# A transformer kernel on one core: the byte offsets of the k-tiles of x^T and of the activations

## The chip, the core and the metric

One core of a Trainium2 chip runs the whole program. Its engines are TensorE (PE in the rows, with its weight loads shown apart as PEld), VectorE (DVE), ScalarE (ACT), GpSimd (POOL) and SyncE (SP), which issues the transfers. The metric is the device time of one execution in microseconds, as the median of a few runs.

## The reference, cut to what matters

Two transformer blocks run one after the other on 256 tokens of width 2048, all in 32-bit floats. Nearly all of the work is products of a token matrix with a large weight matrix:

```
def first_block(x, ...):
    h = rmsnorm(x, pre_mix_g);  proj = h @ w_in          # 2048 -> 4368
    ...two attentions...
    x = x + rmsnorm(concat(o_a, o_b) @ w_out, post_mix_g)
    h = rmsnorm(x, pre_ffn_g)
    u = causal_dwconv(h @ w_up, conv_w, conv_b)          # 2048 -> 11264
    gate, val = split(u)
    x = x + rmsnorm((gelu(gate) * val) @ w_down, post_ffn_g)   # 5632 -> 2048
def second_block(x, c, ctx, ...):
    h  = modulate(rms_norm(x));  hc = modulate(rms_norm(ctx))
    q, k, v, u = h @ w_in_2;     kc, vc = hc @ w_in_2
    x = x + g_a * (concat(attention, pool(u)) @ w_out_2)
    x = x + g_m * (square(relu(modulate(rms_norm(x)) @ w_mlp_up)) @ w_mlp_down)   # 2048 -> 8192 -> 2048
    return rms_norm(x)
```

## The kernel before

Each 32-bit operand is split in two parts of type fp32r, a rounded `hi` and a remainder `lo`, and a product is three matmuls: hi·hi, hi·lo and lo·hi (`products`, L285 is the one line that issues them all). Weights arrive as `raw` tiles, ScalarE makes `hi` from them (L156) and VectorE `lo` (L168).

A matmul has a stationary operand of 128 columns, which a weight load brings into the array ahead of it, and a moving operand, which streams through. Two forms occur in `products`:

- **Form A** (`a_banks`): the weights are stationary (128 columns of them), and a k-tile of the transposed tokens, 256 columns, moves. The groups `up0` to `up10` and `mup0` to `mup7` (the two up-projections), and `kva`, `qa`, `qk0`, `qk1`, `q` are all of this form, with x^T as the moving operand. `ckv` and `kv` are of form A in one half of their work.
- **Form B** (`b_banks`): 128 columns of the token side are stationary, and up to 512 columns of weights move. The groups `dn…` and `mdn…` (the two down-projections) have the activations as their stationary operand, `v`, `u` and the other half of `ckv` and `kv` have x^T, and `wo_a`, `wo_b`, `wo_p` have the attentions' and the pool's outputs.

In both forms the weight load of the next matmul runs while the present matmul streams. A group's matmuls stand in the order k-tile by k-tile, so 24 (form A) or 12 (form B) matmuls in a row use one k-tile of the token side.

x^T (the normalized tokens, transposed) lies in tiles that `xt_tile` hands out: 8 k-tiles of 256 columns each, in a `hi` tile and in a `lo` tile. The tile is 2112 columns wide (8448 bytes in a partition), its k-tiles start at column 16 (64 bytes) and each follows directly on the one before, 1024 bytes on. `make_ht` fills them by ScalarE and VectorE (L364, L365, L374, L375, and L399, L400 for the first four k-tiles). The activations between an up- and a down-projection lie in tiles `[128, 4, 256]` of the pool `p4`, again a `hi` and a `lo`, four k-tiles directly one after the other. They are filled by a pair of instructions for two k-tiles (L960, L961 in the first block, L1346, L1347 in the second).

In the built program every slot of the pools for x^T (8448 bytes), the weights' `hi` and `lo` (4352 bytes) and the activations (4096 bytes) starts at a multiple of 256 bytes in its partition. So before the change the k-tiles of x^T all start 64 bytes past a multiple of 256, and the activations and the weights' columns of `up`, `dn`, `mup` and `mdn` all at a multiple of 256.

The program is written out by hand in one order for each engine. Side work (attention steps, evacuations, the reduction of `w_ada`) is woven in at each `tick`.

Of the kernel before, what the change touches and what calls it, by code (L numbers as in the profile page):

```python
# [9 lines left out]
F32R = mybir.dt.float32r  # L10
# [42 lines left out]
def a_banks(nf, col0=0):  # L53

    return [[("A", 256 * j, col0 + 128 * (i + j)) for j in range(min(2, nf - i))] for i in range(0, nf, 2)]
# [13 lines left out]
class Kernel:  # L69
# [268 lines left out]

    def xt_tile(self):

        return self.A8([128, 2112], F32R)[:, 16:16 + 2048].rearrange("p (k t) -> p k t", t=256)


    def make_ht(self, src, gain, shift=None):
# [272 lines left out]
    def main(self):  # L617
# [313 lines left out]
        def up(g):  # L931
            def after(banks):
                cw = lambda t, f: self.vecs[:, VEC["conv"][0] + 4 * t + f:VEC["conv"][0] + 4 * t + f + 1]
                gs[g] = out = [None, None]
                gv = []

                def taps(s, i):
                    if not gv:
                        gv.extend(self.P4([128, 4, 256]) for _ in range(2))
                    t = 44 * s + 4 * g + i  # L940
                    p = banks[2 * s + i // 2][:, 256 * (i % 2):256 * (i % 2) + 256]
                    d = gv[s][:, i]
                    ac.activation(d, p, AF.Identity, scale=cw(t, 2), bias=cw(t, 3))
                    self.dve.scalar_tensor_tensor(out=d[:, 1:256], in0=p[:, 0:255], scalar=cw(t, 1), in1=d[:, 1:256],
                                                  op0=ALU.mult, op1=ALU.add)
                    self.dve.scalar_tensor_tensor(out=d[:, 2:256], in0=p[:, 0:254], scalar=cw(t, 0), in1=d[:, 2:256],
                                                  op0=ALU.mult, op1=ALU.add)

                def act(i):
                    gate, val = gv[0][:, i:i + 2], gv[1][:, i:i + 2]  # L950
                    j = ac.activation(gate, gate, AF.Gelu_apprx_tanh)
                    if g == 10 and i == 2:
                        self.preload(AF.Exp, j)
                    self.dve.tensor_tensor(out=val, in0=gate, in1=val, op=ALU.mult)

                def split(i):
                    if i == 0:
                        out[:] = [self.P4([128, 4, 256], F32R) for _ in range(2)]
                    val, hi, lo = gv[1][:, i:i + 2], out[0][:, i:i + 2], out[1][:, i:i + 2]
                    ac.copy(hi, val)  # L960
                    self.dve.tensor_tensor(out=lo, in0=val, in1=hi.bitcast(F32), op=ALU.subtract)  # L961

                self.later(*[lambda i=i: (taps(0, i), taps(1, i)) for i in range(4)],
                           *[lambda f=f, i=i: f(i) for i in (0, 2) for f in (act, split)])
            return Group(f"up{g}", 16, 1024, self.loader(a["w_up"], 0, 1024 * g, 1024), a_banks(8), lambda k: ht["xs"](k),
                         before=up_before if g == 0 else None, prep=(lambda b: ht["need"](b + 3)) if g == 0 else None,
                         after=after)
# [364 lines left out]
        def up2(g):  # L1332
            def after(banks):
                gs[g] = hi, lo = [], []

                def split(i):
                    if i % 2 == 0:
                        hi.append(self.P4([128, 4, 256], F32R))
                        lo.append(self.P4([128, 4, 256], F32R))
                    t = self.P2(512)  # L1340
                    t2 = t[:, :512].rearrange("p (j t) -> p j t", j=2)
                    h, l = [x[i // 2][:, 2 * (i % 2):2 * (i % 2) + 2] for x in (hi, lo)]
                    ac.activation(t[:, :512], banks[i], AF.Relu)
                    self.dve.scalar_tensor_tensor(out=t[:, :512], in0=banks[i], scalar=0.0, in1=t[:, :512],
                                                  op0=ALU.max, op1=ALU.mult)
                    ac.copy(h, t2)  # L1346
                    self.dve.tensor_tensor(out=l, in0=t2, in1=h.bitcast(F32), op=ALU.subtract)  # L1347
                self.later(*[lambda i=i: split(i) for i in range(4)])
            return Group(f"mup{g}", 16, 1024, self.loader(a["w_mlp_up"], 0, 1024 * g, 1024), a_banks(8),
                         lambda k: ht["xs"](k), before=up2_before if g == 0 else None,  # L1350
                         prep=(lambda b: ht["need"](b + 3)) if g == 0 else None, after=after)
# [152 lines left out]
```

## Time and profile before

| what | before |
|---|---|
| median of 3 runs | 2154.44 us (2154.38 to 2154.58) |
| the profiled execution, its own time | 2158.41 us |
| its span, first to last instruction | 2156.6 us |
| TensorE busy with matmuls | 2131.0 us, 99% |
| TensorE's weight loads | 1937.7 us, 90% |
| VectorE, ScalarE, GpSimd busy | 73%, 50%, 2% |
| mean granted TensorE clock | 0.997 of full speed (2.4 GHz) |
| HBM read | 484.90 MB, mean 226 GB/s |

A busy TensorE is not TensorE at its peak: matmuls are pipelined and a record is longer than the time until the next one starts. So the number to read is the time from one matmul's start to the next one's, called the pace below. It comes out of rows that give a stretch and the number of matmuls in it.

### The profile page before, as it was taken

The page shows a single profiled execution, that of the slowest core. Times are in us where ns is not written, and L with a number is a line of the kernel's source. Part 1 is how long each engine was busy: PE and PEld are TensorE (multiplying, and loading weights), DVE is VectorE, ACT ScalarE, POOL GpSimd, SP SyncE. Part 2 cuts the span into 40 slices and gives each one's busy share as a digit, 9 for nine tenths or more (in the row PEclk, how much of TensorE's full clock was granted, in tenths as well). Part 3 has the DMA queues.
Part 4 walks back from the last instruction along what each step waited for, and adds up shares of the span by engine and source line. Part 5 has one row for each costly group of instructions (what it writes and reads, how often), then busy time and mean ns, then how long its engine had stood idle before and what let it go on. Part 6 is the DMA issues. An engine that isn't in the chain of part 4 may idle for free.

```text
span 2156.6 us, 35018 instructions
## 1 busy us (share of the span) xinstructions
PE 2131.0 (99%) x14342; PEld 1937.7 (90%) x14342; DVE 1578.7 (73%) x2094; ACT 1076.3 (50%) x1557; POOL 39.3 (2%) x58
## 2 busy tenths in 40 slices
PE   8999999999999999999999999999999999999997
PEld 8998877999998999989989877889898998989986
DVE  6777688788679787797898777765657657555476
ACT  5456565555444543544666466354443434434343
POOL 0001010000000000000000000000000000000000
PEclk9999999999999999999999999999999999999999
DMA  8753575666767788787877744845667677565563
GB/s 310 262 185 129 157 238 211 233 242 243 257 216 249 254 299 306 274 312 259 296 273 267 266 142 141 210 164 187 241 212 273 202 249 252 184 195 188 195 229 104
DMA packets 120641, 490.86 MB, mean 228 GB/s; under 512 B 8673, under 2 KB 12577, under 8 KB 107041
## 3 DMA queue, kind: packets, MB, share of 16 engines
q1 hardware_dynamic: 120480, 488.63, 66.6%
q8 instruction: 112, 1.84, 0.3%
q14 instruction: 49, 0.39, 0.1%
HBM read 484.90 MB, written 2.13 MB: 226 GB/s over the span
## 4 chain that ended last, share of the span: by engine, by line
PE 96%; DVE 2%; DMA 1%; ACT 1%; issue 0%; POOL 0%; POOLq 0%; ACTq 0%; SPq 0%; DVEq 0%
PE b_up L285 23%; PE b_mup L285 17%; PE b_mdn L285 16%; PE b_dn L285 10%; PE b_qk L285 4%; PE b_wo_a L285 4%; PE b_u L285 2%; PE b_v L285 2%; PE b_qa L285 2%; PE b_q L285 2%; PE b_wo_p L285 2%; PE b_wo_b L285 2%; PE b_aux L1160 1%; PE b_kv L285 1%; PE b_ckv L285 1%; PE b_aux L1203 1%
## 5 line engine op out<-in xcount | busy, mean ns | idle before, releaser
L168 DVE TENSOR_TENSOR lo<-raw,hi 128x1024 fp32r<-128x1024 f32 (+2 forms) x716 | 850.3, 1199 | 448.0 <-ACT hi L156 446.2
L156 ACT CAST hi<-raw 128x1024 fp32r<-128x1024 f32 (+2 forms) x716 | 730.1, 1030 | 859.7 <-PE b_up L285 209.0
L285 PE MATMUL b_up<-a,hi 128*128 128x256 f32 x2816 | 499.6, 280 | 0.0
L285 PEld LDWEIGHTS b_up<-a,hi 128*128 128x128 f32 x2816 | 431.3, 188 | 0.3
L285 PE MATMUL b_up<-a,lo 128*128 128x256 f32 x1408 | 393.3, 279 | 0.0
L285 PE MATMUL b_mup<-a,hi 128*128 128x256 f32 x2048 | 363.0, 280 | 1.3 <-ACT a L374 1.3
L285 PE MATMUL b_mdn<-hi,p 128*128 128x512 f32 x1024 | 315.5, 389 | 0.0
L285 PEld LDWEIGHTS b_mup<-a,hi 128*128 128x128 f32 x2048 | 313.2, 187 | 2.1 <-ACT a L374 1.6
L285 PE MATMUL b_mup<-a,lo 128*128 128x256 f32 x1024 | 285.8, 279 | 0.0
L285 PEld LDWEIGHTS b_up<-a,lo 128*128 128x128 f32 x1408 | 265.0, 188 | 0.0
L587 DVE SCALAR_TENSOR_TENSOR raw<-raw,srow 128x2048 f32<-128x2048 f32 x96 | 219.5, 2287 | 27.5 <-DMA raw<-in_w_ada 27.4
L285 PEld LDWEIGHTS b_mdn<-hi,p 128*128 128x128 f32 x1024 | 191.7, 188 | 39.5
L285 PE MATMUL b_dn<-hi,p 128*128 128x512 f32 x704 | 217.1, 390 | 0.0
L285 PE MATMUL b_mdn<-lo,p 128*128 128x512 f32 x512 | 199.2, 389 | 0.0
L285 PEld LDWEIGHTS b_mup<-a,lo 128*128 128x128 f32 x1024 | 192.5, 188 | 0.0
L285 PEld LDWEIGHTS b_dn<-hi,p 128*128 128x128 f32 x704 | 131.6, 188 | 26.8
L285 PE MATMUL b_dn<-lo,p 128*128 128x512 f32 x352 | 137.1, 390 | 1.0 <-DVE lo L168 1.0
L285 PEld LDWEIGHTS b_mdn<-lo,p 128*128 128x128 f32 x512 | 96.1, 188 | 20.1
L285 PE MATMUL b_qk<-a,hi 128*128 128x256 f32 x512 | 93.4, 283 | 0.0
L285 PE MATMUL b_wo_a<-hi,a 128*128 128x512 f32 x256 | 80.3, 395 | 0.0
L285 PEld LDWEIGHTS b_qk<-a,hi 128*128 128x128 f32 x512 | 77.7, 188 | 2.6 <-issue 2.0
L285 PEld LDWEIGHTS b_dn<-lo,p 128*128 128x128 f32 x352 | 66.1, 188 | 15.2 <-DVE lo L168 1.4
(264 smaller groups left out, 2543.3 us busy)
## 6 DMA issues: line engine op xcount, KB each, us to landing
raw<-in_w_ada SPq DMA_DIRECT2D x96, 1024.0 KB, 5.6
raw<-in_w_up SPq DMA_DIRECT2D x88, 1024.0 KB, 5.0
raw<-in_w_mlp_up SPq DMA_DIRECT2D x64, 1024.0 KB, 5.0
raw<-in_w_mlp_down SPq DMA_DIRECT2D x64, 1024.0 KB, 5.6
raw<-in_w_in SPq DMA_DIRECT2D x50, 1024.0 KB, 6.0
raw<-in_w_down SPq DMA_DIRECT2D x44, 1024.0 KB, 5.9
raw<-in_w_out SPq DMA_DIRECT2D x32, 512.0 KB, 6.6
raw<-in_w_out SPq DMA_DIRECT2D x16, 1024.0 KB, 6.1
```

What stands on the lines that cost most here:

```text
L156: nc.scalar.copy(h, r)
L168: self.dve.tensor_tensor(out=l, in0=r, in1=h.bitcast(F32), op=ALU.subtract)
L285: self.mm = self.pe.matmul(dst, lhsT, rhs, start=first and n == 0 and m == 0, stop=last and n == len(prog) - 1 and m == 2, skip_group_chec ...
L587: self.dve.scalar_tensor_tensor(out=r, in0=r, scalar=1.0, in1=self.srow[0], op0=ALU.mult, op1=ALU.mult, accum_out=self.ada[:, f:f + 1])
L1160: self.pe.matmul(bk[:, 256 * m:256 * m + 256], x, k[:, 512 * m + o:512 * m + o + 256], start=n == 0 and m == 0, stop=n == 1 and m == 1, sk ...
L1203: self.pe.matmul(o[64 * s:64 * s + 64, 128 * qt:128 * qt + 128], v[:, c:c + 64], PT[x][:, 128 * kt:128 * kt + 128], start=kt == 0, stop=kt ...
```

## The change

The k-tiles of x^T start at column 32 (128 bytes past the slot's start) and each lies 260 columns (1040 bytes) after the one before. So they start at 128, 144, 160, ... 240 bytes past a multiple of 256. The tile keeps its width of 2112 columns. The activations' four k-tiles start at 0, 16, 32 and 48 bytes past a multiple of 256, in tiles that are now 1088 columns wide, so a slot of the pool `p4` becomes 4352 bytes, again a multiple of 256.

```
     def xt_tile(self):
-        return self.A8([128, 2112], F32R)[:, 16:16 + 2048].rearrange("p (k t) -> p k t", t=256)
+        return self.A8([128, 2112], F32R)[:, 32:].rearrange("p (k t) -> p k t", t=260)[:, :, 0:256]
+
+    def act_tile(self):
+        return self.P4([128, 1088], F32R)[:, :1040].rearrange("p (k t) -> p k t", t=260)[:, :, 0:256]
...
                 def split(i):                       # up: first block
                     if i == 0:
-                        out[:] = [self.P4([128, 4, 256], F32R) for _ in range(2)]
+                        out[:] = [self.act_tile() for _ in range(2)]
...
                 def split(i):                       # up2: second block
                     if i % 2 == 0:
-                        hi.append(self.P4([128, 4, 256], F32R))
-                        lo.append(self.P4([128, 4, 256], F32R))
+                        hi.append(self.act_tile())
+                        lo.append(self.act_tile())
```

Every engine has the same instructions in the same order, with the same waits, before and after. Other than addresses, the only thing that differs in an instruction is the pattern of 80 writes on ScalarE and 80 on VectorE, which now leave a gap of 16 bytes between two k-tiles. The pools behind `p4` move up by 2304 bytes, nine times 256.

## Rows read from the trace of the kernel before

**Rows 1.** The page: busy us, share of the span, instructions of each engine.

```profile
PE 2131.0 (99%) x14342; PEld 1937.7 (90%) x14342; DVE 1578.7 (73%) x2094; ACT 1076.3 (50%) x1557; POOL 39.3 (2%) x58
```

**Rows 2.** What TensorE waited for: us in total, times, longest us.

```profile
PE b_warm L318 <- DMA a<-in_x: 6.0, 1, 6.0
PE b_aux L357 <- DVE a L433: 2.9, 2, 2.5
...
PE b_aux L1160 <- DVE a L1269: 0.3, 1, 0.3
```

**Rows 3.** The chain that ended last, in order of time: start us, us, what.

```profile
65.32 11.30 PE b_kva L285 x96
...
1171.29 45.23 PE b_q L285 x384
...
1614.74 43.56 PE b_mdn L285 x192
1658.30 45.23 PE b_mup L285 x384
```

**Rows 4.** Groups of matmuls on TensorE: shapes, xcount | busy us, mean ns of one.

```profile
L285 PE MATMUL b_up<-a,hi 128*128 128x256 f32 x2816 | 499.6, 280 | 0.0
...
L285 PE MATMUL b_mup<-a,hi 128*128 128x256 f32 x2048 | 363.0, 280 | 1.3 <-ACT a L374 1.3
...
L285 PE MATMUL b_mdn<-hi,p 128*128 128x512 f32 x1024 | 315.5, 389 | 0.0
...
L285 PE MATMUL b_dn<-hi,p 128*128 128x512 f32 x704 | 217.1, 390 | 0.0
```

**Rows 5.** Timeline of TensorE in `qk1`, x^T moving, one stretch of 27 matmuls.

```profile
194.98 0.28 PE L285 MATMUL b_qk<-a,lo 128*128 128x256 f32 x1
195.09 0.39 PE L285 MATMUL b_qk<-a,hi 128*128 128x256 f32 x2
...
197.47 0.39 PE L285 MATMUL b_qk<-a,hi 128*128 128x256 f32 x2
...
198.04 0.28 PE L285 MATMUL b_qk<-a,lo 128*128 128x256 f32 x1
```

**Rows 6.** The same group 41 us later, a stretch of 15 matmuls.

```profile
238.77 0.28 PE L285 MATMUL b_qk<-a,lo 128*128 128x256 f32 x1
238.89 0.40 PE L285 MATMUL b_qk<-a,hi 128*128 128x256 f32 x2
...
240.54 0.28 PE L285 MATMUL b_qk<-a,lo 128*128 128x256 f32 x1
```

**Rows 7.** Timeline of `u`, x^T stationary, a stretch of 9 matmuls.

```profile
1239.83 0.63 PE L285 MATMUL b_u<-hi,a 128*128 128x512 f32 x2
...
1241.93 0.39 PE L285 MATMUL b_u<-hi,a 128*128 128x512 f32 x1
```

**Rows 8.** Timeline of `v`, x^T stationary, three banks of three matmuls.

```profile
27.27 0.49 PE L285 MATMUL b_v<-hi,a 128*128 128x352 f32 x2
27.60 0.32 PE L285 MATMUL b_v<-lo,a 128*128 128x352 f32 x1
27.76 0.49 PE L285 MATMUL b_v<-hi,a 128*128 128x352 f32 x2
```

**Rows 9.** Stretches `up0`-`up2`, `up3`-`up4`, one `mup`: length, busy by engine, then clock.

```profile
372.00:515.50 143.50, 141.75 (x1187) 141.51 (x1188) 118.89 (x151) 75.10 (x99) 0.54 (x1) 0.99 0.65 229
557.60:649.70 92.10, 92.10 (x777) 91.79 (x776) 66.29 (x74) 43.11 (x51) 0.00 (x0) 1.00 0.67 234
1569.50:1614.70 45.20, 45.20 (x386) 45.20 (x385) 22.11 (x21) 19.38 (x23) 0.00 (x0) 1.00 0.65 217
```

**Rows 10.** Writes of k-tiles on ScalarE: with gaps already (L399), and without (L374, L1346).

```profile
L1346 ACT CAST p<-p 128x512 fp32r<-128x512 f32 x32 | 19.8, 620 | 11.0 <-DVE p L1344 11.0
L374 ACT CAST a<-p 128x512 fp32r<-128x512 f32 x24 | 14.1, 621 | 11.5 <-DVE p L371 11.5
...
L399 ACT CAST a<-p 128x512 fp32r<-128x512 f32 x2 | 1.2, 618 | 0.6 <-DVE p L398 0.5
```

## Prediction

> **What bounds the kernel now.** The page comes first: TensorE is busy 99% of the span, VectorE 73%, ScalarE 50% [rows 1]. The view of waits says that this is no average over starved stages: the longest wait is the one for the first input, 6.0 us, and the nine kinds of wait in that view come to some 15 us in all [rows 2]. So for 2140 us TensorE is limited by itself, and the question is how fast one matmul follows another. A record's length does not tell this (280 ns and 389 ns, while the next one starts long before [rows 4]). The chain in order of time does. It has a `mup` group of 384 matmuls, x^T moving, in 45.23 us, which is 117.8 ns each, and the same figure for `q`; `kva` has 11.30/96 = 117.7 ns. An `mdn` pair has 192 matmuls in 43.56 us, or 226.9 ns each [rows 3]. The granted clock is 1.00, the 2.4 GHz level, in the stretches of the up-projections [rows 9], and I take it for all. At that level 256 columns take 106.7 ns and 512 take 213.3 ns. So form A carries 11.1 ns beyond its streaming and form B 13.6 ns.
>
> The timeline shows what the 11.1 ns are. In `qk1` there is a stretch in which 27 matmuls of form A follow each other in 198.04 - 194.98 = 3.06 us, that is 113.3 ns each [rows 5], and 41 us later, with the same tiles' offsets and the same shapes, 15 matmuls take 240.54 - 238.77 = 1.77 us, 118.0 ns each [rows 6]. So form A has two paces, 113.3 and 117.8 ns, and a run of matmuls stays in one until something interrupts it; the first stretch crosses from one k-tile to the next (at 197.47) without losing its pace. 113.3/106.7 is 1.062 and 226.9/213.3 is 1.064: the down-projections are at the fast pace of their form already, the up-projections are at the slow one throughout.
>
> Form B has a slow pace too. In `u`, where x^T is stationary, nine matmuls of 512 columns take 1241.93 - 1239.83 = 2.10 us, 233.3 ns each [rows 7], 6.4 ns more than in `mdn`. The shapes are the same. What differs is that the stationary tile starts 64 bytes past a multiple of 256 in `u`, and at a multiple in `mdn`, the moving weights being at a multiple in both. In `v`, again with x^T stationary, three matmuls of 352 columns take 27.76 - 27.27 = 0.49 us, 163.3 ns each, 16.7 ns over their 146.7 ns of streaming [rows 8]. I read these rows so: the stream of the moving operand and the weight load that runs beside it can get into each other's way or miss each other, and the offset between the two decides which of the two paces a run settles in.
>
> **The change, part by part.** No instruction, wait or transfer is added, removed or moved, so every term is a pace times a count.
>
> *x^T as the moving operand.* The groups that are steadily slow are `up` (2816 + half as many = 4224 matmuls) and `mup` (2048 + 1024 = 3072) [rows 4], `qa` and `q` (384 each) and `kva` (96): 8160 matmuls. At the fast pace each saves 117.8 - 113.3 = 4.45 ns (before rounding), in all 36.3 us. Whether the new offsets give the fast pace, no row shows, since no matmul of before has a moving operand at another offset than 0, 64 or 128. From both sides: the best pace that any row shows for 256 columns is 113.3 ns, so the gain ends at 36.3 us; the worst excess is that of `v`, 16.7 ns instead of 11.1 ns, which would cost 5.6 x 8160 = 46 us. I take the full gain, for this reason: the fast pace exists at the offset that is worst placed now, and it persists once entered [rows 5]. The change gives a group eight offsets in turn, 24 matmuls each, and one offset that lets a run slip into the fast pace would carry the k-tiles behind it as well.
>
> *x^T as the stationary operand.* `u` (192 matmuls, at most 6.4 ns each, 1.2 us), `v` (288 matmuls) and the halves of `ckv` and `kv` may gain or lose 1 to 3 us. `qk0` and `qk1`, `ckv` and `kv` are part fast and part slow and may gain some 2 us. I take nothing for all of these; they lie inside the range.
>
> *The activations.* `dn` and `mdn` hold (704 + 1024) x 1.5 = 2592 matmuls [rows 4], now with the stationary tile 0, 16, 32 or 48 bytes past the multiple. They are at the fast pace, and no row of form B is below it, so there is nothing to gain that a row shows. The loss is bounded by `u`: 6.4 ns on the three k-tiles in four that leave offset 0, 1944 x 6.4 = 12.4 us, or 16.6 us if the fourth is dragged along. I take nothing: the first k-tile of each four is still at offset 0, where the fast pace is reached, and in `qk1` that pace outlives a change of k-tile.
>
> *The writes.* 160 instructions now write with a gap. L399 does so already and takes 618 ns, against 620 and 621 ns for L1346 and L374 that write without one [rows 10]: nothing.
>
> *What a faster TensorE runs into.* In `up0` to `up2` VectorE is busy 118.89 of 143.5 us [rows 9]. With 1152 x 4.45 = 5.1 us less that is 86% of the stretch; in the later groups 66.29 of 88.7 us, 75%; in `mup` about half. Should this cover fail, the loss is at most the gain of the stretch itself, 5.1 us.
>
> The sum, against the profiled execution (2158.4 us, of which 2156.6 us are its span): 2158.4 - 36.3 = 2122.1 us. The median of the runs lies 4.0 us below that execution, so **2118 us** is forecast.
>
> **A rule against it.** The slow pace [rows 6, 7] and the fast one [rows 3, 5] stand side by side for the same shapes and weights' offsets. The Trainium skill ("TensorE: Matmul & The Clock Gate", Part 2, step 1) says that TensorE reads its streaming operand and its weight loads through two independent ports, so that loading the next weights "doesn't steal SBUF read bandwidth from the running matmul". By that rule an offset can do nothing, and the time stays at 2154. The trace speaks against it so far, since `u` and `mdn` differ in nothing else that I can find.
>
> **The rivals.**
> - *No effect, 2154 us, chance 0.14.* The paces are set by what a run of matmuls came from (the two stretches of `qk1` have the same offsets [rows 5, 6]), and the long groups get into the slow one whatever the offset. For it: 64 bytes is the only offset that form A shows. Against it: `u` against `mdn`. The rule of the skill above ends here too.
> - *Part of the gain, 2125 to 2149 us, chance 0.18.* Some of the eight offsets are fast and others slow: half of the k-tiles give 2154.4 - 18 = 2136 us. The full gain with the down-projections slowed gives 2118 + 12 = 2130 us.
> - *Slower through the down-projections, 2167 us, chance 0.17.* The x^T side keeps its pace, and the activations at 16, 32 and 48 bytes fall into the pace of `u`: 2154.4 + 12.4. For it: form B leaves the fast pace at 64 bytes, and nothing says where between 0 and 64 that begins. It decides once more than a third of the 36.3 us fails to come (12.4 us).
> - *Slower through x^T, 2160 to 2199 us, chance 0.09.* The new offsets bring form A the excess of `v`, up to 46 us. Against it: the excess of `v` is form B's.
>
> **How the numbers follow.** The forecast, all long groups of form A at 113 ns and `dn`, `mdn` unchanged, has chance 0.42 and a range of its own of 2112 to 2123 us (the 2 to 6 us of the parts taken at nothing). Faster by over 0.2%, which is 4 us and about what a measurement of this kernel can tell from no change: 0.42 + 0.18 = 0.60. Within it: 0.14. Slower: 0.17 + 0.09 = 0.26. The range from 2112 to 2168 us takes in the forecast's, the partial gain, no effect and about half of the slower down-projections, together about 0.8.
>
> **What would show it.** In the chain of the changed kernel a `mup` group should read 43.5 us instead of 45.23, and an `mdn` pair stay at 43.56; two `b_mup` matmuls in a row should span 0.39 us, as at the fast pace [rows 5], and not 0.40, as at the slow one [rows 6]. The timeline of one group shows whether the pace changes with the k-tile, every 24 matmuls. The prediction is wrong if `mup` stays at 45.2 us (no effect), if `mdn` goes toward 192 x 233 ns = 44.8 us, or if TensorE waits for VectorE's `lo` (L168) in `up0` to `up2`.

## The result and the profile after

The changed kernel takes 2169.46 us (median of 4 runs, 2168.11 to 2170.28), the kernel before 2154.41 us (4 runs, 2154.14 to 2154.58): a ratio of 1.0066, 95% interval 1.0053 to 1.0079. Instead of the 36 us that were forecast as a gain there is a loss of 15 us. Its profiled execution took 2169.87 us, with a span of 2168.1 us, 11.5 us more than the span of before. (The profiled execution of before lay 4.0 us above its own median, that of after only 0.4 us, so the two traces show 11.5 of the 15 us.)

The page's line of the engines, of after (busy us, share, instructions), answers to [rows 1]:

```profile
PE 2143.6 (99%) x14342; PEld 1943.3 (90%) x14342; DVE 1579.7 (73%) x2094; ACT 1076.3 (50%) x1557; POOL 38.9 (2%) x58
```

The counts are the same, VectorE and ScalarE are busy as long as before, TensorE 12.6 us longer. The view of waits of after, TensorE's two longest and the last row of the view, against [rows 2]:

```profile
PE b_warm L318 <- DMA a<-in_x: 6.0, 1, 6.0
PE b_aux L361 <- DVE a L437: 2.9, 2, 2.5
...
PE b_ckv L285 <- DVE lo L168: 0.3, 1, 0.3
```

No wait of any size is new. The clock is not it either: a `mup` stretch has the granted clock at 1.00, the 2.4 GHz level, in after as in before [rows 9] (the stretch, its length, busy us of PE, PEld, DVE, ACT and POOL, then the clock):

```profile
1575.40:1620.80 45.40, 45.40 (x386) 45.40 (x385) 22.10 (x21) 19.37 (x23) 0.00 (x0) 1.00 0.64 216
```

So the loss is in the pace, and the chain of after (start us, us, what), against [rows 3], says in which groups:

```profile
65.06 11.37 PE b_kva L285 x96
...
516.21 44.19 PE b_dn L285 x192
560.39 90.83 PE b_up L285 x768
...
1176.56 45.40 PE b_q L285 x384
...
1620.86 44.19 PE b_mdn L285 x192
1665.05 45.43 PE b_mup L285 x384
```

An `mdn` pair went from 43.56 to 44.19 us, 226.9 to 230.2 ns a matmul, and `dn` reads the same; for 2592 matmuls that is 0.63 x 2592/192 = 8.5 us. A `mup` group went from 45.23 to 45.43 us, 0.52 ns a matmul; over the 8160 matmuls of the long groups of form A that is 4.2 us, an estimate from `mup` alone. Together 12.7 us, against 11.5 us by the spans.

The timeline of an `mdn` half in after shows that the pace changes with the k-tile. One product is a row "hi,p x2" and a row "lo,p x1", and four products (12 matmuls) use one k-tile:

```profile
1620.70 0.62 PE L285 MATMUL b_mdn<-hi,p 128*128 128x512 f32 x2
...
1623.46 0.61 PE L285 MATMUL b_mdn<-hi,p 128*128 128x512 f32 x2
...
1626.19 0.62 PE L285 MATMUL b_mdn<-hi,p 128*128 128x512 f32 x2
...
1628.98 0.63 PE L285 MATMUL b_mdn<-hi,p 128*128 128x512 f32 x2
...
1631.78 0.62 PE L285 MATMUL b_mdn<-hi,p 128*128 128x512 f32 x2
...
1634.53 0.61 PE L285 MATMUL b_mdn<-hi,p 128*128 128x512 f32 x2
```

Read from row to row: the k-tile at offset 0 takes 2.76 us (230 ns a matmul), the one at 16 bytes 2.73 us (227.5), the one at 32 bytes 2.79 us (232.5), the one at 48 bytes 2.80 us (233.3). The next is at 0 again, and this time takes 2.75 us (228.4 by the starts in ns). In the k-tile at 16 bytes the matmul starts give eleven steps of 226.7 ns and one of 235.0, the last, which leads into the k-tile at 32 bytes: behind offset 0 it keeps the pace of before.

In `mup` the same view, over two k-tiles at 192 bytes of one group, the fifth (from 1676.34) and the thirteenth (from 1699.05), and the one at 208 bytes behind the latter; each pair of rows "hi x2", "lo x1" is one product:

```profile
1676.34 0.40 PE L285 MATMUL b_mup<-a,hi 128*128 128x256 f32 x2
...
1679.16 0.40 PE L285 MATMUL b_mup<-a,hi 128*128 128x256 f32 x2
...
1699.40 0.39 PE L285 MATMUL b_mup<-a,hi 128*128 128x256 f32 x2
...
1701.78 0.40 PE L285 MATMUL b_mup<-a,hi 128*128 128x256 f32 x2
...
1702.14 0.40 PE L285 MATMUL b_mup<-a,hi 128*128 128x256 f32 x2
...
1704.64 0.40 PE L285 MATMUL b_mup<-a,hi 128*128 128x256 f32 x2
```

From 1699.40 to 1701.78 there are 21 matmuls in 2.38 us, 113.3 ns each; from 1702.14 to 1704.64 there are 21 in 2.50 us, 119.0 ns. So one of the eight offsets did let a run into the lower pace, as the prediction had it, and the run lost it with its k-tile. It did not let every run in: in the fifth k-tile, at 192 bytes too and behind one at 176 bytes like the thirteenth, 24 matmuls take 2.82 us, 117.5 ns each. By the matmul starts it is the same in 17 of the 19 groups of `up` and `mup`; in `up0` and `mup0` neither k-tile gets there. Over all of `mup` in after, matmul starts set against the program's addresses give these means per offset: 119.2 ns at 128 bytes, 118.8 at 144, 118.1 at 160, 119.3 at 176, 116.1 at 192, 119.3 at 208, 118.2 at 224 and 117.8 at 240. Before, at 64 bytes, it was 117.8. (The last two k-tiles of a group do not stand one after the other: the program alternates between them, six matmuls of each in form A and three in form B, so the means at 224 and 240 bytes are partly those of a mixture.)

Below, *lower pace* is 113.3 ns for 256 columns and 226.7 ns for 512.

### The profile page after: what moved, and what is told of

The parts are those of the page before. It is cut to its first block, busy times and chain, and to the rows that moved or that the text cites. A ratio compares the mean times of both kernels' runs of the same rounds, so it can differ in the third digit from the quotient of the medians.

```text
span 2168.1 us, 35018 instructions
## 1 busy us (share of the span) xinstructions
PE 2143.6 (99%) x14342; PEld 1943.3 (90%) x14342; DVE 1579.7 (73%) x2094; ACT 1076.3 (50%) x1557; POOL 38.9 (2%) x58
## 4 chain that ended last, share of the span: by engine, by line
PE 97%; DVE 1%; ACT 1%; POOL 0%; DMA 0%; issue 0%; POOLq 0%; ACTq 0%; SPq 0%; DVEq 0%
PE b_up L285 23%; PE b_mup L285 17%; PE b_mdn L285 16%; PE b_dn L285 11%; PE b_qk L285 4%; PE b_wo_a L285 4%; PE b_u L285 2%; PE b_v L285 2%; PE b_q L285 2%; PE b_qa L285 2%; PE b_wo_p L285 2%; PE b_wo_b L285 2%; PE b_aux L1164 1%; PE b_ckv L285 1%; PE b_kv L285 1%; PE b_aux L1207 1%
```

## The experiments

My theory after the result: each operand's byte offset, modulo 256, decides which paces are open to a run, for each k-tile anew. The rivals: a run carries the pace that it has reached into the next offset (the prediction's reason); the two halves of the change hurt only together; the loss is in the gapped writes and not in the offsets.

### Each half of the change alone

`acts_only` keeps x^T as before, `xt_only` keeps the activations as before:

```
 # acts_only: act_tile() as in the change, and
 def xt_tile(self):
     return self.A8([128, 2112], F32R)[:, 16:16 + 2048].rearrange("p (k t) -> p k t", t=256)
 # xt_only: P4([128, 4, 256], F32R) as before, and
 def xt_tile(self):
     return self.A8([128, 2112], F32R)[:, 32:].rearrange("p (k t) -> p k t", t=260)[:, :, 0:256]
```

> Only the activations' k-tiles are spread (0, 16, 32, 48 bytes); x^T keeps its 64 bytes. Theory O (the offset of the k-tile in use sets the pace of the matmuls that use it): an mdn pair reads 44.19 us as in the changed kernel (0.63 more than before), a mup group 45.23 as before, and the time is 2154.4 + 13.5 pairs x 0.63 = 2163 us. Rival N (the activations were not touched by the offset, and the loss comes from x^T by another way): mdn 43.56 us, time 2154 us.

> Only x^T is spread (128 to 240 bytes); the activations stay at a multiple of 256. Theory O: a mup group reads 45.43 us, an mdn pair 43.56, the time is 2154.4 + 19 x 0.2 + under 1 for the other groups = 2158 to 2159 us. Rival N: 2169 us.

`acts_only` took 2162.78 us (6 runs), 1.0033 of before [1.0021, 1.0046]; `xt_only` 2162.17 us (5 runs), 1.0032 [1.0019, 1.0044]; before, beside them, 2155.31 us. So +7.5 and +6.9 us, whose sum, 14.3, is the loss of the whole change within its interval: the halves add up. The chain of `acts_only`:

```profile
649.14 44.19 PE b_dn L285 x192
693.33 90.45 PE b_up L285 x768
...
1173.11 43.53 PE b_q L285 x384
...
1571.36 45.23 PE b_mup L285 x384
1616.59 44.19 PE b_mdn L285 x192
```

Only `dn` and `mdn` moved, by 8.5 us. `q` is a surprise: its x^T is at 64 bytes as before, and yet it reads 43.53 us here, 113.4 ns, where before has 45.23 (and in `kick1`, below, it reads 43.52). So 64 bytes admits both paces even for a whole group, and an execution may come out 1.7 us shorter by that alone. The chain of `xt_only` shows the reverse:

```profile
828.58 90.83 PE b_up L285 x768
...
1617.43 43.56 PE b_mdn L285 x192
1660.99 45.43 PE b_mup L285 x384
```

Here `mdn` is untouched and `mup` reads as in the whole change: 4.2 us by the chain, 6.9 us by the runs, 3 to 4 us above the time that was expected. The other 2.7 us lie within the executions of before (its profiled one was 4.0 us above its median), and which group of theirs is quicker there is not shown.

### Scanning the offset

`scan1` to `scan5` give each section of the program one uniform offset in place of a stepped one (x^T in all five, the activations in the first two). Each number in a list is a byte offset:

```
+XT = [0, 192, 64, 128, 240]          # scan1: kva/qa/qk/v, up, ckv, kv/q/u, mup
+ACT1 = [16, 16, 32, 32, 48, 48, 64, 64, 0, 0, 0]; ACT2 = [80, 96, 112, 128, 144, 160, 176, 192]
-    def xt_tile(self):
-        return self.A8([128, 2112], F32R)[:, 16:16 + 2048].rearrange("p (k t) -> p k t", t=256)
+    def xt_tile(self, o):
+        return self.A8([128, 2112], F32R)[:, o // 4:o // 4 + 2048].rearrange("p (k t) -> p k t", t=256)
+    def act_tile(self, o):
+        return self.P4([128, 1088], F32R)[:, o // 4:o // 4 + 1024].rearrange("p (k t) -> p k t", t=256)
 # scan2: XT 16, 0, 64, 32, 160; ACT1 208, 224, 240, 8, 4; ACT2 12, 20, 24, 28, 40, 44, 56, 0
 # scan3: XT 48, 192, 64, 80, 208; scan4: 96, 176, 64, 112, 224; scan5: 104, 144, 64, 108, 116 (activations at 0)
```

> Every group has one offset for all its k-tiles, laid directly one after the other: x^T 0 bytes for v, kva, qa and qk, 192 for up, 64 for ckv, 128 for kv, q and u, 240 for mup; the activations 16, 32, 48, 64 and 0 bytes for the five pairs of dn and 80, 96, 112, 128, 144, 160, 176, 192 for the eight of mdn. Theory O: the pace is constant in a group and belongs to its offset: up at 192 bytes about 116 ns or, if it locks, 113.3 (groups of 44.5 or 43.5 us instead of 45.23), mup at 240 about 117.8, dn at 0 and 16 bytes 43.6 us a pair, at 32 and 48 near 44.6 us. Theory S (spreading itself, the change of offset from k-tile to k-tile, is what costs): all groups of one offset read as before, 45.23 and 43.56 us, whatever the offset.

> As the scan before, with x^T at 16 bytes for v, kva, qa and qk, 0 for up, 64 for ckv, 32 for kv, q and u, 160 for mup; the activations 208, 224, 240, 8 and 4 bytes for dn and 12, 20, 24, 28, 40, 44, 56 and 0 for mdn. Theory O: mup at 160 bytes about 118.0 ns (45.3 us), dn at 4 and 8 bytes near 43.6 us a pair if 16 is still at the lower pace, mdn at 0 bytes 43.56 us, at 40 to 56 near 44.6. If the pace depends on the offset modulo 128 alone, up at 0 bytes has the pace that q has at 128 bytes in the other scan. Theory S: 45.23 and 43.56 us throughout.

> The activations stay at a multiple of 256, so every dn and mdn ends at 226.7 ns, and x^T has one offset for all its k-tiles: 48 bytes for v, kva, qa, qk, 192 for up, 64 for ckv, 80 for kv, q, u, 208 for mup. Theory H (at an offset that admits both paces, the one that a group keeps is fixed by how the run enters it, so by the group ahead): up at 192 has the same pace in all groups that follow a dn at offset 0, either 117.8 or 113.3 ns throughout (45.23 or 43.52 us a group; the time 2154 or about 2135), not a mixture as in the first scan, where the dn ahead had offsets of 16 to 64. Theory O, the offset alone sets it: the mixture stays.

> As the scan before, with x^T at 96 bytes for v, kva, qa, qk, 176 for up, 64 for ckv, 112 for kv, q, u and 224 for mup. Theory H: each offset has one pace throughout up and mup, between 116 and 120 ns where no run reaches the lower pace; a group of 43.5 us shows an offset at which a run that comes from dn at offset 0 gets there by itself.

> One offset for each x^T, the activations at a multiple of 256: 104 bytes for v, kva, qa, qk, 144 for up, 64 for ckv, 108 for kv, q, u and 116 for mup. If the lower pace at 112 belongs to a neighbourhood of that offset, mup at 116 and q at 108 show 113.4 ns as well; if it belongs to that offset alone, as form B's lower pace belongs to 0 (at 4 and 8 bytes it was 230 to 233 ns), they read 116 to 120 ns. up at 144 bytes: 116 to 120 ns, 44.5 to 46 us a group.

Their single times (2165.53, 2182.21, 2160.91, 2166.8 and 2170.33 us) mix good and bad offsets; what they are for is the pace of each section. For form A, from the chains and the starts of matmuls (ns for 256 columns):

| offset of x^T | 0 | 16 | 32 | 48 | 64 | 80 | 96 | 104 | 108 | 112 |
|---|---|---|---|---|---|---|---|---|---|---|
| pace | 120.0 | 116.7 | 117.8 | 118.3 | 117.8 or 113.3 | 118.4 | 120.0 | 120.1 | 120.0 | **113.4** |

| offset of x^T | 116 | 128 | 144 | 160 | 176 | 192 | 208 | 224 | 240 |
|---|---|---|---|---|---|---|---|---|---|
| pace | 121.7 | 118.7 | 118.7 or 116.7 | 118.7 | 119.3 | 117.8 or 113.4 | 119.2 | 118.3 | 117.2 |

For form B (ns for 512 columns): 226.7 at offset 0 and nowhere else; 228.4 to 230.1 at 24, 44, 176, 192 and 240; 230.7 to 235 at every other offset tried (4 to 224).

Rows of the chains show what the scan was for. In `scan1` all of `up` is at 192 bytes, and pairs with the same addresses modulo 256 read two paces, 117.8 and 113.4 ns:

```profile
561.31 90.45 PE b_up L290 x768
...
696.56 87.06 PE b_up L290 x768
```

`scan3` asked whether the way into a group decides at 192 bytes, with every `dn` at offset 0. `up1` and `up2`, directly behind `up0`, read 113.4 ns, and all four pairs behind a `dn` read 117.8 ns, as theory H expected:

```profile
408.51 103.38 PE b_up L288 x912
...
555.42 90.45 PE b_up L288 x768
```

In `scan1` the pairs behind a `dn` at 16 and at 64 bytes read 117.8 ns, those behind one at 32 and at 48 bytes 113.4. So the group ahead fits as what decides there; with one pair for each of these offsets that is a lead and not shown. In `scan5`, at 144 bytes, `up` has two paces as well, 118.7 ns up to `up2` and 116.7 ns in the eight groups after it:

```profile
410.35 108.23 PE b_up L288 x912
...
562.13 89.60 PE b_up L288 x768
```

In `scan2`, with `up` at 0 bytes (120.0 ns) and the activations of `dn` at 224 (233.3 ns):

```profile
653.97 44.80 PE b_dn L290 x192
698.77 92.15 PE b_up L290 x768
```

In `scan4`, with `q` at 112 bytes, 113.4 ns from end to end:

```profile
1179.95 43.55 PE b_q L288 x384
```

What follows: of the change's eight offsets for x^T, one alone (192) admits the lower pace, five are above the 117.8 ns of before, and 144 can be on either side. Of its four offsets for the activations, one (0) is the best; the other three, taken uniformly, read 233 ns, 16 bytes too, where the expectation had the lower pace. The spreading (theory S) and the gapped writes are not what costs: with one offset for all k-tiles, and no gap, the paces are as slow or slower. And 0 and 128 bytes differ (120.0 and 118.7 ns), so the offset modulo 128 does not tell the pace.

### A break ahead of a group

Does what came before a run choose its pace at 64 bytes? `kick1` keeps all offsets of before and cuts one matmul of the first k-tile of a group into two, at another column in each group:

```
+                cut, at = KICK.get(self.group, (0, 0))      # "up10": (80, 0), "mup1": (32, 2), ...
+                if first and op == ("A", 0, 0) and cut and m == at:
+                    self.pe.matmul(dst[:, :cut], lhsT, rhs[:, :cut], start=m == 0, stop=False, ...)
+                    dst, rhs = dst[:, cut:], rhs[:, cut:]
```

> All offsets as before. In each up and mup group but the first of either, one matmul of the first k-tile is cut in two (32 to 224 columns and the rest), on the first pass in up and on the third in mup, which adds one weight load and changes nothing but the instant at which the next matmul starts. Theory H (64 bytes admits both paces and the way in decides): some of the 17 groups read 43.5 to 43.7 us and the others 45.2 to 45.4, and each stays in its pace to its end. Theory O (the offset alone sets the pace): all 17 read 45.2 to 45.4 us, the cut's weight load added.

It took 2154.85 us beside 2153.91 us of before, one run each. One of its 17 cut groups changed its pace, `up10`, and the uncut rest of it stayed there for all 383 matmuls:

```profile
960.38 45.12 PE b_up L295 x383
1005.70 43.44 PE b_up L295 x383
```

So at one offset a pace, once entered, does last over sixteen k-tiles; but a break of this kind is no handle on it: 16 groups of 17 stayed at 117.8 to 118.0 ns. That is against theory O, which had all 17 at the slow pace, and agrees with H. But `q`, which nothing was done to, reads 43.52 us in this run and 45.23 in before, so the break need not be what moved `up10`.

### x^T at 112 bytes

The scan points to one version better than both kernels. `xt112` differs from before in one number:

```
-        return self.A8([128, 2112], F32R)[:, 16:16 + 2048].rearrange("p (k t) -> p k t", t=256)
+        return self.A8([128, 2112], F32R)[:, 28:28 + 2048].rearrange("p (k t) -> p k t", t=256)
```

> One number is changed against the kernel before: x^T starts 112 bytes past a multiple of 256 instead of 64, its k-tiles directly one after the other, the activations untouched. In the scan, q ran at 113.4 ns at this offset. If 112 bytes is an offset at which runs get into the lower pace by themselves: all groups of form A read 43.5 us for 384 matmuls, mdn 43.56 us a pair, and the time is 2154 - 36 = 2118 us. If q got there by its way in alone (theory H): up and mup keep a pace of 116 to 120 ns, 2150 to 2170 us.

It took **2120.27 us** (5 runs, 2119.06 to 2121.9) against 2155.49 us of before (9 runs): 0.9841 [0.9827, 0.9854], 35.2 us less. The page and the chain of it:

```profile
PE 2093.4 (99%) x14342; PEld 1900.0 (90%) x14342; DVE 1576.4 (74%) x2094; ACT 1078.8 (51%) x1557; POOL 40.0 (2%) x58
```

```profile
63.91 10.94 PE b_kva L285 x96
...
548.70 87.08 PE b_up L285 x768
...
1147.95 43.55 PE b_q L285 x384
...
1540.98 43.56 PE b_mup L285 x384
1584.53 43.55 PE b_mdn L285 x192
```

All long groups of form A read 113.4 to 114 ns, and the down-projections are untouched. The gain is the 36.3 us of the prediction's sum, to about a microsecond. The granted clock of a `mup` stretch is 1.00 here too:

```profile
1541.00:1584.50 43.50, 43.50 (x385) 43.50 (x385) 22.01 (x20) 19.24 (x23) 0.00 (x0) 1.00 0.68 228
```

Nor does the load of the engines beside set the pace: in before VectorE is busy 83% of `up0` to `up2`, 72% of `up3` and `up4` and 49% of a `mup` [rows 9], and all three read 117.8 ns. The prediction's cover held as well: in `up0` to `up2` of `xt112` VectorE is busy 118.34 of 139.6 us, 85%, and the view of waits has no wait of TensorE for a `lo` above 0.4 us:

```profile
365.50:505.10 139.60, 137.13 (x1188) 136.37 (x1187) 118.34 (x150) 76.64 (x104) 0.54 (x1) 0.99 0.65 231
```

### Does a pace carry over from one offset to the next?

`half112` puts k-tiles 0 to 3 of each tile of x^T at 64 bytes, which admits both paces, and k-tiles 4 to 7 at 112 bytes:

```
+        return self.A8([128, 2112], F32R)[:, 16:16 + 2072].rearrange("p (h m) -> p h m", m=1036)[:, :, 0:1024]
+            .rearrange("p h (k t) -> p h k t", t=256)
-            return his[k // 8][:, k % 8], los[k // 8][:, k % 8]
+            return his[k // 8][:, k % 8 // 4, k % 4], los[k // 8][:, k % 8 // 4, k % 4]
```

> x^T's k-tiles 0 to 3 of each tile at 64 bytes, 4 to 7 at 112, the activations as before. Theory 'the offset decides, k-tile by k-tile': 113.4 ns on the four k-tiles at 112 and 117.8 ns on the four at 64, so a mup group and q read 192 x 117.8 + 192 x 113.4 = 44.4 us, an up pair 88.8 us, and the time is half of the way to x^T all at 112, about 2154.4 - 17.5 = 2137 us. Theory of my prediction, 'a run that has reached the lower pace carries it on': a group's first k-tiles at 64 come from another form and stay at 117.8, but k-tiles at 64 that come directly behind k-tiles at 112 (k-tiles 8 to 11 of a group's 16, and 0 to 3 of the second group of a pair) read 113.4 ns too; a mup group then reads 96 x 117.8 + 288 x 113.4 = 44.0 us, an up pair 87.5 us, and the time is about 2128 us.

It took 2139.11 us (4 runs) against 2154.12 us, 0.9923 [0.9906, 0.9939]: 15.0 us less, near the 17.5 us without carrying and far from the 26 us with it. A `mup` group reads 44.43 us and `q` 44.38. The timeline of `q` shows the changes of offset, from 64 to 112 bytes at 1171.61, from 112 back to 64 at 1182.49, and to 112 again at 1193.79:

```profile
1171.25 0.40 PE L285 MATMUL b_q<-a,hi 128*128 128x256 f32 x2
...
1171.61 0.39 PE L285 MATMUL b_q<-a,hi 128*128 128x256 f32 x2
...
1182.49 0.40 PE L285 MATMUL b_q<-a,hi 128*128 128x256 f32 x2
...
1193.79 0.39 PE L285 MATMUL b_q<-a,hi 128*128 128x256 f32 x2
```

Three matmuls take 0.36 us up to 1171.61. The next 96, at 112 bytes, take 10.88 us, 113.3 ns each, and the 96 after them, at 64 bytes, 11.30 us, 117.7 ns each. The change comes with the k-tile in both directions. From 112 to 64 bytes nothing is carried, though 64 bytes would admit it.

That is not so for every step: in the changed kernel the k-tile of the activations at 16 bytes keeps the lower pace behind the one at 0, in all but its last step, while uniformly at 16 bytes `dn` reads 233.3 ns (`scan1`). So a pace may pass to the next offset or not; of the steps that were looked at, 0 to 16 passes it on, and 16 to 32, 192 to 208 and 112 to 64 do not.

### Is it the difference of the two offsets?

In every kernel so far the weights of these groups start at a multiple of 256. `wscan` leaves x^T at 64 bytes and shifts the weights' tiles, and puts the activations of the second block at 64 as well:

```
+WOFF = {'up': 208, 'mup': 64, 'q': 112, 'dn': 208, 'mdn': 64};  ACT2 = [64] * 8
-                hi = self.w_p.tile([128, 1088], F32R, tag="hi", name=f"hi{self.n}")[:, :w]
+                hi = self.w_p.tile([128, 1088], F32R, tag="hi", name=f"hi{self.n}")[:, o:o + w]   # lo alike
```

> x^T stays at 64 bytes and the activations of the first block at 0; the weights' hi and lo tiles are shifted instead: 208 bytes in up and dn, 64 in mup and mdn, 112 in q; the activations of the second block are at 64. Theory 'only the difference of the two offsets counts' (token side less weights, modulo 256): up has 112 and reads 113.4 ns (an up pair 87.1 us), mup has 0 and reads 120.0 ns (46.1 us a group), q has 208 and reads 119.2 (45.8 us), dn has 48 and reads 233.3 ns (44.8 us per 192), mdn has 0 and reads 226.7 ns (43.56 us). Theory 'the token side's own offset counts, the weights' does nothing': up, mup and q stay at 117.8 ns (90.5, 45.2, 45.2 us), dn stays at 226.8 (43.56 us) and mdn goes to 233.3 (44.8 us). Theory 'both offsets count, each in its own way': other numbers than these.

Its one time is 2180.05 us. The chain:

```profile
653.05 45.05 PE b_dn L291 x192
698.10 92.16 PE b_up L291 x768
...
1186.22 45.23 PE b_q L291 x384
...
1586.11 46.07 PE b_mup L291 x384
1632.18 43.55 PE b_mdn L291 x192
```

For form B the lower pace goes with equal offsets, as far as these two groups tell: with both operands at 64 bytes `mdn` is back at 226.8 ns, which `dn` in `scan1` does not reach at 64 with the weights at 0 (233.3), and `dn` leaves it once the weights alone move to 208. But it reads 234.6 ns there, and a difference of 48 bytes read 233.3 with the weights at 0: that the difference is all that counts is not shown. For form A `mup` has difference 0 and reads 120.0 ns, as at 0 against 0. But `up`, with difference 112, reads 120.0 ns and not 113.4, and `q`, with difference 208, 117.8 and not 119.2. So in form A the weights' offset counts too, and not through the difference alone: neither simple theory stands there. What `wscan` says of `q` is the weakest of these, since 117.8 ns is also what `q` reads with the weights at 0.

## Why the prediction was wrong, point by point

- **The bound, right.** TensorE's own pace sets the time: no wait of any size was added, and the paces of the long groups, 12.7 us, account for the 11.5 us between the spans (the rest, 1.2 us, is of the other sign).
- **That the operands' offsets matter, right; that the offset between the two decides which of two paces a run settles in, not borne out.** One number moved by 12 columns, nothing else, takes 35.2 us off (`xt112`). But form A shows more than two paces (113.4 to 121.7 ns), the difference of the offsets does not set its pace (`wscan`), and at 64, 144 and 192 bytes the same offset has two. The Trainium skill ("TensorE: Matmul & The Clock Gate", Part 2, step 1) has two independent ports, so that a weight load takes nothing from the running matmul; no effect would follow from it, and the runs show effects of either sign up to 1.6%. What part the weight load has in them was not tried, so the prediction's reading, a moving operand and a weight load in each other's way, stays a guess.
- **"One offset that lets a run slip into the fast pace would carry the k-tiles behind it as well": the step that failed.** The first half came true in part (192 bytes, 113.3 ns, in one of a group's two k-tiles there), the second did not: the run lost its pace at the next k-tile, at 208 bytes (119.0 ns), and `half112` shows the same from 112 to 64 bytes. What I had seen in `qk1`, a pace that outlives a change of k-tile [rows 5], were k-tiles at one and the same offset. `kick1` and `scan1` confirm that over sixteen k-tiles and more; it says nothing of a step of 16 bytes. The other premise, that 64 bytes "is worst placed now", had no row behind it and was wrong as well: twelve of the 18 other offsets in the scan read only paces above its 117.8 ns. So the term of -36.3 us became +4.2 us by the chain.
- **"I take nothing" for the activations: mis-sized, and for the same reason.** Offsets 32 and 48 run at 232.5 and 233.3 ns, and offset 0, which should have held the fast pace, loses some 2 to 3 ns in getting back to it (230 ns behind `mup`, 228.4 behind 48 bytes). Only 16 bytes does what the prediction hoped for: 227.5 ns behind offset 0, where it runs at 233.3 if all k-tiles are at 16 (`scan1`). In all 8.5 us, inside the 12.4 us that the prediction gave as the bound.
- **The rival that came.** It ended at 2167 us: x^T keeps its pace, the activations fall to that of `u`. That is the case, with 8.5 instead of 12.4 us there, and some 4 to 7 us on the x^T side that this rival did not have.
- **Right at nothing:** the writes with a gap cost nothing (VectorE 1579.7 and ScalarE 1076.3 us busy), and VectorE's cover holds at the lower pace too.

What stays open: why just 112 bytes (form A, weights at a multiple of 256) and equal offsets (form B) give the lower pace; what chooses between two paces at 64, 144 and 192 bytes, for which the way into a group is a lead (`scan1`, `scan3`); and most offsets of form A that are no multiple of 16.

## What to carry to other kernels

Where TensorE is busy 99% and waits for nothing, divide a group's time in the chain by its matmuls and set it against the best stretch of the same shape: 117.8 against 113.3 ns left 4% to be had in these groups, and one column offset in a tile's view gave it. Try such an offset uniformly, section by section, before stepping it: a stepped offset averages over good and bad ones, and a pace seen to persist at one offset need not survive the step to the next. When a trace has no row for the resource that a change touches, the chance of the hoped-for case should not rest on an extrapolation of a single stretch.

## What the runs showed that was not expected

- The pace of 256-column matmuls goes from 113.4 to 121.7 ns by the moving operand's offset alone, and four bytes beside the best (108: 120.0 ns, 116: 121.7 ns) all of it is gone.
- The two lower paces are one: 113.33/256 and 226.67/512 are both 0.4427 ns a column, 17/16 of a period of the 2.4 GHz clock. No group of `products` with 256 or 512 columns read below that in any run.
- One offset can hold two paces for a whole group with the same instructions (`up` at 192 bytes: 90.45 and 87.06 us; `q` at 64: 45.23 and 43.53 us), and two k-tiles of one group can differ the same way (the fifth and the thirteenth of `mup` after the change). A single profile of one group is then no measure of its offset.
